# Seven block products in place of eight in six of the eight feed-forward blocks of both MLPs, and eight of fourteen modulation blocks moved into the attention

## The chip, the cores and the metric

One Trainium2 chip, one of its cores. The kernel is one launch. The metric is the device time of an execution in microseconds (us), read as the median of several executions. TensorE (PE) does the matrix products, VectorE (DVE), ScalarE (ACT) and GpSimd (POOL) the element-wise work, and SyncE (SP) issues nearly all DMA transfers from its own queue.

## What is computed

A two-layer trunk over 512 tokens of width 1024, batch 1, all in float32. Each layer is a token mixer and then an MLP, and each of these four sub-layers n = 0..3 is modulated by a vector c:

```python
shift, scale, gate = split(silu(c) @ ada_w[layer, s] + ada_b[layer, s], 3)   # gate is 1 + gate
u = x * (1.0 + scale) + shift
y = square(relu(u @ mlp_w1[layer] + mlp_b1[layer])) @ mlp_w2[layer] + mlp_b2[layer]   # s == 1: the MLP
x = layer_norm(ALPHA * x + gate * y, ln_g[layer, s], ln_b[layer, s])
```

`mlp_w1` is 1024 x 4096, `mlp_w2` 4096 x 1024, `ada_w[layer, s]` 1024 x 3072. The mixer of layer 0 joins a gated recurrence and linear attention heads. The mixer of layer 1 is an attention of 16 heads of 64 with a forget gate.

## The kernel before

**Products in three parts.** Every operand of a large product is held as a pair: `hi`, the float32 value rounded to the `fp32r` type (a copy on ACT), and `lo`, what the rounding left (a subtraction, mostly on DVE). A product is three matmuls, hi·hi, hi·lo and lo·hi, accumulated in PSUM (`mm3`). Each of them has a stationary operand of 128x128 and, in the MLPs, a moving one of 128x512.

**Stages in order of time.** The even mixer, its output projection (`mix_out(0)`), `mlp(0)`, the attention (`fox`), `mix_out(1)`, `mlp(1)`.

**An MLP.** `up(b)` makes block b of eight: 512 of the 4096 hidden channels for all 512 tokens, 4 groups f of 128 channels, each 24 matmuls. ACT takes relu and square from PSUM (`r`, then `hh`), DVE squares once more (`h2`) and subtracts for `hl`. `down(b)` multiplies these 512 tokens x 512 channels with rows b·512 to b·512+511 of `mlp_w2`, 96 matmuls of 128x512, and DVE adds the eight results from PSUM to `Y`. The order is up(0), then up(b), down(b-1) in turn, then down(7).

**Weights.** `plan_weights` lists all weight blocks of 1 MB in the order of use. `w_pre` loads the next ones to one of two staging tiles (`ws`, `WS_BUFS`) and splits one block: ACT writes `wh`, DVE `wl`. The split pairs stand in a rotation of four tiles each of 128x1024 (tags `wh`, `wl` of pool `wp`), or, for every second pair of blocks (`wsmall`, set by `alternate`), as 128x512 tiles from the general pool `s2`, which has 42 tiles (`S2_BUFS`). A third pool, `u8`, has eight tiles of 128x4x512.

**Modulation.** A block is 512 columns of one `ada_w[layer, s]`, a job (n, cb). `ada_steps` is a generator over jobs, four pieces each. A piece is two DMA loads of 128x512 (`ast`) and two multiply-adds into `acc`. There are two generators, stepped together by `tick()`: "v" does its multiply-adds on DVE (SCALAR_TENSOR_TENSOR, the first of a job TENSOR_SCALAR), "g" scales on ACT and adds on POOL. Two pieces into the next job, `finish` sums over the partitions with matmuls against ones (`pada`). Where `halved` is set the sum is first split in a pair (`acch`, `accl`), except for the last job of a generator. Shift and scale rows go through DRAM (`mod_d`), gates stay in SBUF for n = 1 and 3 and go through DRAM for n = 2 (`gate_d`). Six jobs run in the even mixer. Of the other fourteen, twelve run in mlp(0) and two, the gate of n = 3, in mlp(1), started at b = 1.

**Attention.** `fox` walks through 16 heads with the orders "aduntu3uv" and the like: a is the scores and softmax of the next head, d the decay tables (`Dm`, POOL) two heads ahead, n the normalisation (POOL), t the transposes of the probabilities (`ppt`, then `Ph` on ACT and `Pl` on DVE), v the values, digits the stacking of q and k. u is `run()`: one of 52 projection units (36 for q, k and v of head groups 1 to 3, each 24 matmuls of 128x256, then 16 for the gate, 12 of 128x512 each), which fill PE between the small products of the heads. The residual tables are prepared in single steps by `step()`, which takes from `self.later`.

**Order.** The program order above gives priorities. When the program is built a planner lays out, for each engine, a fixed order: the earliest work in program order whose inputs and tiles are free by its own estimates. On the chip each engine and the SP queue follow that order and wait at semaphores.

Of the kernel before, what the change touches and what calls it, by code (L numbers as in the profile page):

```python
# [36 lines left out]
PRED = mybir.dt.uint32  # L37

# [35 lines left out]
class Trunk:  # L74
# [26 lines left out]
    def setup(self):  # L101
        nc, i, c = self.nc, self.i, self.const
        self.ident = c.tile([P, P], F32, name="ident")
        make_identity(self.tc.nc, self.ident)
        self.ones = c.tile([P, P], F32, name="ones")
        nc.vector.memset(self.ones, 1.0)
        self.ones_r = c.tile([P, P], F32R, name="ones_r")
        nc.vector.tensor_copy(self.ones_r, self.ones)
        self.eps = c.tile([P, 1], F32, name="eps")
        nc.gpsimd.memset(self.eps, LN_EPS)  # L110

        crow = c.tile([KC, P], F32, name="crow")
# [21 lines left out]
        self.gate_d = {2: self.dram.tile([1, D], F32, name="gated2")}  # L134
# [79 lines left out]
    def ada_steps(self, jobs, eng, halved):  # L214
# [22 lines left out]
        def finish(n, cb, *acc):  # L237
# [8 lines left out]
            else:  # L246
                h = cb - 4
                if n == 2:
# [7 lines left out]
                if n == 2:  # L256
                    nc.sync.dma_start(self.gate_d[n][:, h * 512:h * 512 + 512], g)
# [58 lines left out]
    def plan_weights(self):  # L316
# [5 lines left out]

        def out(w, n):
# [4 lines left out]
        def mlp(l):  # L328
            w1, w2 = i["mlp_w1"][l], i["mlp_w2"][l]
            up = lambda b: [("ch", w1, b * 512, 256), ("ch", w1, b * 512 + 256, 256)]  # L330
            dn = lambda b: [("rows", w2, b * 512, 2 * l + 1), ("rows", w2, b * 512 + 256, 2 * l + 1)]
            L.extend(up(0))
# [3 lines left out]

        self.wsmall = set()

        def alternate(n0):
            for q in range(n0, len(L)):  # L340
                if (q - n0) // 2 % 2:
                    self.wsmall.add(q)

        n0 = len(L)
        out(i["ev_w_out"][0], 0)
        mlp(0)
        alternate(n0)
# [7 lines left out]
        out(i["od_w_out"][0], 2)  # L355
        mlp(1)
        alternate(n0)
# [3 lines left out]
    def w_dma(self):  # L361
        d = self.wlist[self.n_dma]
        kind, w = d[0], d[1]
        if kind == "ch":
# [34 lines left out]
    def w_pre(self, eng=None):  # L399
# [8 lines left out]
        kind = d[0]  # L408
        small = self.n_split in self.wsmall
# [18 lines left out]
        self.n_split += 1  # L428

# [668 lines left out]
    def mlp(self, l, X, rest, last):  # L1098
# [4 lines left out]
        def up(b):  # L1103
            hh, hl = self.u8("hh"), self.u8("hl")
            ws = self.w_take() + self.w_take()
# [10 lines left out]
            for f in range(4):  # L1116
                if b == 0:
# [3 lines left out]
                if f % 2 == 0:  # L1121
                    self.w_pre()
                col = 64 + l * 32 + b * 4 + f
                r, h2 = self.s2("r"), self.s2("h2")
                nc.scalar.activation(r, pts[f], AF.Relu, bias=self.colA[:, col:col + 1])
                nc.scalar.activation(hh[:, f], r, AF.Square)
                nc.vector.tensor_tensor(h2, r, r, op=ALU.mult)
                nc.vector.tensor_tensor(hl[:, f], h2, hh[:, f].bitcast(F32), op=ALU.subtract)
                if b:
                    self.step(2)  # L1130
                    if f % 2:
                        self.tick()
            return hh, hl

# [44 lines left out]
        Y = [[self.s2(f"Y{t}_{h}") for h in range(2)] for t in range(NT)]  # L1179
        prev = up(0)  # L1180
        for b in range(1, nb):
            if b == 1 and last:
                self.ada = [self.ada_steps([(3, 4)], "g", True), self.ada_steps([(3, 5)], "v", True)]
            cur = up(b)
            down(b - 1, *prev)
            prev = cur
        self.tick(99)
# [55 lines left out]
    def fox(self, rest):  # L1243
# [252 lines left out]
        def run(k=1):  # L1496
            for _ in range(k):
                f = next(units, None)
                if f:
                    f()  # L1500

# [57 lines left out]
    def run(self):  # L1559
# [3 lines left out]
        self.ada = [self.ada_steps([(1, 4), (2, 0), (2, 2), (2, 4), (3, 0), (3, 2)], "g", True),  # L1563
                    self.ada_steps([(1, 5), (2, 1), (2, 3), (2, 5), (3, 1), (3, 3)], "v", True)]
# [32 lines left out]
```

## Time and profile before

| | |
|---|---|
| median of three runs | 1263.32 us (1262.36 to 1264.07) |
| the profiled execution: its own time, its span | 1266.51 us, 1264.8 us |
| matmuls on PE | 6543, busy 1224.6 us |
| DVE, ACT, POOL busy | 908.8, 590.2, 512.9 us |
| HBM read | 172.10 MB |

All times in a row are us from the start of the span unless marked ns. Rows come from one profiled execution of the kernel before. In the trace every instruction carries one line, that of a helper (L50), so groups are told apart by the names of their tiles: `out<-in`.

### The profile page before, as it was taken

Reading aid. Unit: us, or ns where it says so; the run is one execution under the profiler, and the core shown is the slowest. Engines: PE = TensorE matmul, PEld = TensorE weight load, DVE = VectorE, ACT = ScalarE, POOL = GpSimd, SP = SyncE. Lnnn points to the kernel's source line nnn. Section 1 sums busy time; section 2 is a strip of 40 time slices with the busy share of each in tenths; the row PEclk is TensorE's granted clock in tenths of the full one; section 3 lists DMA queues with packets and bytes.
Section 4 is the critical chain, followed back from the end, with each engine's and each line's share of the span. In section 5 each row is a group of like instructions: output and inputs, shape, how many; then the busy total and the mean of one; then the engine's idle time right before and its main releaser. Section 6 shows DMA issues by size and latency. Waiting matters only on the chain. (4 is left out here: it accounts for less than half of the span.)

```text
span 1264.8 us, 17847 instructions
## 1 busy us (share of the span) xinstructions
PE 1224.6 (97%) x6543; PEld 1044.2 (83%) x6543; DVE 908.8 (72%) x1423; ACT 590.2 (47%) x1044; POOL 512.9 (41%) x524
## 2 busy tenths in 40 slices
PE   6999899999999999999999999999899999999997
PEld 5787678888888888888999999887888788888886
DVE  7689898768877866879578878778768744543656
ACT  3476653452453544432567767753453342322321
POOL 3665523346330321474266558558437000000166
PEclk9999999999999999999999999999999999999999
DMA  9657416163666466524232332343262624232311
GB/s 316 186 199 267 173 61 198 56 230 119 240 224 233 145 195 227 182 67 124 81 101 85 92 93 52 113 153 106 79 233 72 211 67 133 81 117 70 133 34 67
DMA packets 126409, 177.52 MB, mean 140 GB/s; under 512 B 9270, under 2 KB 82644, under 8 KB 126322
## 3 DMA queue, kind: packets, MB, share of 16 engines
q1 hardware_dynamic: 126210, 176.33, 42.4%
q8 instruction: 52, 0.85, 0.3%
q14 instruction: 35, 0.29, 0.1%
q10 hardware_dynamic: 112, 0.05, 0.0%
HBM read 172.10 MB, written 4.26 MB: 139 GB/s over the span
## 5 line engine op out<-in xcount | busy, mean ns | idle before, releaser
L50 DVE TENSOR_TENSOR wl<-ws,wh 128x512 fp32r<-128x512 f32 (+1 forms) x255 | 269.3, 1081 | 67.7 <-ACT wh L50 63.4
L50 ACT CAST wh<-ws 128x1024 fp32r<-128x1024 f32 (+2 forms) x271 | 207.5, 808 | 200.5 <-PE p L50 81.4
L50 PE MATMUL p<-uh,wh 128*128 128x512 f32 (+1 forms) x576 | 206.2, 366 | 0.0
L50 PE MATMUL p<-uh,wl 128*128 128x512 f32 (+1 forms) x576 | 205.9, 365 | 0.0
L50 PE MATMUL p<-wh,hh 128*128 128x512 f32 (+1 forms) x516 | 201.0, 390 | 0.0
L50 PE MATMUL p<-wh,hl 128*128 128x512 f32 (+1 forms) x516 | 200.0, 388 | 0.0
L50 PE MATMUL p<-wl,hh 128*128 128x512 f32 (+1 forms) x516 | 199.9, 387 | 0.0
L50 PE MATMUL p<-ul,wh 128*128 128x512 f32 (+1 forms) x576 | 192.9, 366 | 0.0
L50 POOL TENSOR_TENSOR acc<-acc,ast 128x512 f32<-128x512 f32 x70 | 102.9, 1470 | 203.3 <-ACT ast L50 108.4
L50 DVE TENSOR_TENSOR h<-r 128x512 f32<-128x512 f32 x64 | 53.6, 840 | 123.6 <-ACT r L50 123.6
L50 PEld LDWEIGHTS p<-uh,wl 128*128 128x128 f32 x576 | 108.6, 189 | 17.5
L50 PEld LDWEIGHTS p<-uh,wh 128*128 128x128 f32 x576 | 108.6, 189 | 17.6
L50 PEld LDWEIGHTS p<-ul,wh 128*128 128x128 f32 x576 | 100.9, 189 | 17.4
L50 PEld LDWEIGHTS p<-wh,hh 128*128 128x128 f32 x516 | 96.9, 188 | 20.3 <-issue 0.2
L50 PEld LDWEIGHTS p<-wl,hh 128*128 128x128 f32 x516 | 96.9, 188 | 20.2 <-issue 0.5
L50 PEld LDWEIGHTS p<-wh,hl 128*128 128x128 f32 x516 | 96.9, 188 | 19.8
L50 ACT ACTIVATE r<-p,colA 128x512 f32<-128x512 f32 x64 | 43.8, 684 | 148.7 <-PE p L50 148.7
L50 POOL TENSOR_TENSOR ws<-ws,gate 128x512 f32<-128x512 f32 x16 | 25.0, 1597 | 210.6 <-DMA ws<-in_mlp_w_dram 210.6
L50 DVE TENSOR_TENSOR Y<-Y,p 128x512 f32<-128x512 f32 x96 | 64.8, 681 | 41.0 <-PE p L50 40.3
L50 ACT ACTIVATE ast<-ast,cs 128x512 f32<-128x512 f32 x70 | 49.9, 721 | 91.3 <-DMA ast<-in_ada_w_dram 91.3
L50 DVE SCALAR_TENSOR_TENSOR acc<-ast,cs,acc 128x512 f32<-128x512 f32 x70 | 82.5, 1179 | 13.2 <-DMA ast<-in_ada_w_dram 12.7
L50 POOL TENSOR_TENSOR ul<-u,uh 128x512 fp32r<-128x512 f32 x32 | 45.0, 1418 | 74.0 <-ACT uh L50 65.4
(320 smaller groups left out, 2681.2 us busy)
## 6 DMA issues: line engine op xcount, KB each, us to landing
ws<-in_mlp_w_dram SPq DMA_DIRECT2D x64, 1024.0 KB
ast<-in_ada_w_dram SPq DMA_DIRECT2D x160, 256.0 KB
ws<-in_od_w_in_dram SPq DMA_DIRECT2D x16, 1024.0 KB
ast<-in_ada_w_dram SPq DMA_DIRECT2D x16, 512.0 KB
ws<-in_ev_w_in_dram SPq DMA_DIRECT2D x7, 1024.0 KB
ws<-in_ev_w_out_dram SPq DMA_DIRECT2D x4, 1024.0 KB
nf<-fd SPq DMA_DIRECT2D x16, 256.0 KB
ws<-in_od_w_out_dram SPq DMA_DIRECT2D x4, 1024.0 KB
```

Source lines behind the costliest of these rows:

```text
L50: x = f(*a, **k)
```

## The change

The pairs of blocks (0,1), (2,3), (4,5) of both MLPs take a new path (`WINOGRAD = (0, 1)` lists the layers). `up(b, raw=True)` keeps the squares as plain float32 (`hr`), with no `h2` and no `hl`. Two such tiles, 512 tokens x 1024 channels, are cut in 2x2 blocks of 256 tokens x 512 channels, and the 1024 x 1024 piece of `mlp_w2` in 2x2 blocks of 512 x 512. `winograd` multiplies seven combinations of them (Winograd's form of Strassen's scheme), each 4 x 2 x 3 = 24 matmuls of 128x512. `factor` makes the left operands (S1 to S4 by sums in place) and splits them. `wino_b` makes the right ones (T1 to T4 by sums in place in four `s2` tiles `wE` and in a staging tile) and splits them. `wino_dma` loads block B22 twice, once into `wE`. The seven results are accumulated in 12 `s2` tiles over the three pairs and put together by 8 additions per MLP. Blocks 6 and 7 go the old way, as up(6), up(7), down(6), down(7). The residual steps run one to a group from b = 2. The W1 blocks of the new path are split in the rotation of four, but for up(1) (and, as before, some of the last blocks).

The jobs (2,4), (2,5) and (3,0) to (3,5) are stepped in the attention, one tick to two projection units from the second `run()` on. mlp(0) keeps six jobs, mlp(1) none. All gates go through DRAM.

```diff
+WINOGRAD = (0, 1)
+WINO_B = ("B11", "T3", "T1", "T2", "B21", "T4", "B22")
+WINO_A = ("A11", "S3", "S1", "S2", "A12", "A22", "S4")
...
+            if l in WINOGRAD:
+                for g in range(0, 6, 2):
+                    L.extend(up(g) + up(g + 1) + [("wino", w2, g * 512, x) for x in WINO_B])
+                L.extend(up(6) + up(7) + dn(6) + dn(7))
...
+        if which in WINO_SRC:
+            r, c = WINO_SRC[which]
+            st = self.wp.tile([P, 4, 512], F32, tag="ws", bufs=WS_BUFS, name="ws")
+            nc.sync.dma_start(st, block(r0 + 512 * r, 512 * c))
+        if which == "T3":
+            E = [self.s2(f"wE{k}") for k in range(4)]
+            for k in range(4):
+                nc.sync.dma_start(E[k], w[r0 + 512 + k * P:r0 + 512 + k * P + P, 512:1024])
...
+        elif which == "T3":
+            self.wE, self.wB12 = self.wE_next, st
+            for k in range(4):
+                sub(self.wE[k], self.wE[k], st[:, k])
+        if which == "T1":
+            for a in (0, 2):
+                x = self.wB12[:, a:a + 2, :]
+                sub(x, x, self.wB11[:, a:a + 2, :])
+                r += halves(self.wB12, a)
+            for k in range(4):
+                nc.vector.tensor_tensor(self.wE[k], self.wE[k], self.wB11[:, k], op=ALU.add)
+            return r
+        for a in (0, 2):
+            r += halves(self.wE if which in ("T3", "T2", "T4") else st, a)
+        if which == "B21":
+            for k in range(4):
+                sub(self.wE[k], st[:, k], self.wE[k])
...
+            if q % 3 < 2:
+                t = self.u8("ha", F32R, (2, 4, 256))
+                parts = [(slice(0, 4), t[:, 0], t[:, 1])]
+            else:
+                parts = [(slice(f, f + 2), *[self.s2(x, F32R).rearrange("p (k t) -> p k t", k=2) for x in ("hah", "hal")])
+                         for f in (0, 2)]
+            if name == "S3":
+                sub(a[1], a[0], a[1])
+            elif name == "S1":
+                sub(a[1], a[3], a[1])
+                nc.vector.tensor_tensor(a[0], a[0], a[1], op=ALU.add)
+            elif name == "S4":
+                sub(a[2], a[2], a[1])
...
+            for fs, hi, lo in parts:
+                nc.scalar.copy(hi, src[:, fs])
+                sub(lo, src[:, fs], hi.bitcast(F32))
...
+            plan = [("1", False, "U2", None), ("7", False, "Q7", None), ("5", False, "Q5", 1), ("6", False, "U2", None),
+                    ("1", True, "C11", 0), ("7", True, "D21", 0), ("5", True, "D12", 1)]
+            for q, (bank, on, to, bias) in enumerate(plan):
+                if len(ops) < min(q + 3, 7):
+                    ops.append(factor(WINO_A[len(ops)], H, len(ops)))
+                w = self.w_take()
+                self.w_pre()
...
+            for g in range(0, 6, 2):
+                H = [up(g, True)[0], None]
+                first = [factor(WINO_A[q], H, q) for q in range(2)]
+                H[1] = up(g + 1, True)[0]
+                winograd(g, acc, H, first)
...
+                    done.append(f)
+                    if len(done) % 2 == 0:
+                        self.tick()
+
+        done = []
+        self.ada = [self.ada_steps([(2, 4), (3, 0), (3, 2), (3, 4)], "g", True),
+                    self.ada_steps([(2, 5), (3, 1), (3, 3), (3, 5)], "v", True)]
...
-        self.ada = [self.ada_steps([(1, 4), (2, 0), (2, 2), (2, 4), (3, 0), (3, 2)], "g", True),
-                    self.ada_steps([(1, 5), (2, 1), (2, 3), (2, 5), (3, 1), (3, 3)], "v", True)]
+        self.ada = [self.ada_steps([(1, 4), (2, 0), (2, 2)], "g", True),
+                    self.ada_steps([(1, 5), (2, 1), (2, 3)], "v", True)]
```

## Rows read from the trace of the kernel before

**Rows 1.** The page: busy time of the engines, then busy tenths in 40 slices

```profile
PE 1224.6 (97%) x6543; PEld 1044.2 (83%) x6543; DVE 908.8 (72%) x1423; ACT 590.2 (47%) x1044; POOL 512.9 (41%) x524
...
PE   6999899999999999999999999999899999999997
...
DVE  7689898768877866879578878778768744543656
```

**Rows 2.** Windows, by stage: busy us of each engine (instructions), clock, DMA share, GB/s

```profile
178.00:240.00 62.00, 59.26 (x298) 49.43 (x298) 54.64 (x89) 26.98 (x49) 17.58 (x11) 1.00 0.44 145
...
280.00:540.00 260.00, 260.00 (x1148) 215.16 (x1147) 198.28 (x226) 116.96 (x181) 86.32 (x59) 1.00 0.57 190
...
638.00:772.00 134.00, 133.63 (x1076) 131.28 (x1075) 107.45 (x266) 96.64 (x204) 83.34 (x156) 1.00 0.29 86
772.00:858.00 86.00, 83.81 (x468) 72.43 (x467) 65.22 (x134) 52.76 (x114) 52.16 (x74) 1.00 0.35 117
904.00:1251.00 347.00, 345.73 (x1609) 288.79 (x1609) 191.44 (x252) 116.65 (x181) 84.41 (x61) 1.00 0.32 106
```

**Rows 3.** Windows of 20 us, same columns: 140:160, 880:900, 980:1000

```profile
140.00:160.00 20.00, 15.86 (x92) 12.14 (x92) 17.30 (x29) 12.77 (x24) 9.16 (x7) 0.91 0.25 82
...
880.00:900.00 20.00, 16.74 (x75) 13.57 (x74) 18.46 (x36) 8.77 (x18) 11.31 (x6) 0.91 0.46 151
...
980.00:1000.00 20.00, 18.73 (x78) 14.20 (x77) 15.12 (x20) 12.21 (x20) 2.91 (x2) 1.00 0.66 232
```

**Rows 4.** The chain that ended last: start us, us, what

```profile
995.14 255.74 PE p L50 x1128
```

**Rows 5.** Groups of DVE, 1000 to 1180 us, POOL idle: busy us, mean ns

```profile
L50 DVE TENSOR_TENSOR wl<-ws,wh 128x512 fp32r<-128x512 f32 x39 | 24.7, 685 | 0.0
L50 DVE TENSOR_TENSOR Y<-Y,p 128x512 f32<-128x512 f32 x35 | 23.9, 685 | 24.1 <-PE p L50 23.5
L50 DVE TENSOR_TENSOR wl<-ws,wh 128x1024 fp32r<-128x1024 f32 x16 | 19.6, 1222 | 7.6 <-ACT wh L50 7.0
```

**Rows 6.** Timeline of DVE in mlp(1): start us, us for all instructions of the row

```profile
999.67 3.10 DVE L50 TENSOR_TENSOR wl<-ws,wh 128x512 fp32r<-128x512 f32 x5
```

**Rows 7.** Groups of DVE, 280 to 540 us (mlp(0))

```profile
L50 DVE SCALAR_TENSOR_TENSOR acc<-ast,cs,acc 128x512 f32<-128x512 f32 x42 | 48.3, 1150 | 10.1 <-DMA ast<-in_ada_w_dram 9.7
L50 DVE TENSOR_TENSOR wl<-ws,wh 128x512 fp32r<-128x512 f32 x48 | 46.2, 979 | 3.7 <-ACT wh L50 3.7
...
L50 DVE TENSOR_SCALAR acc<-ast,cs 128x512 f32<-128x512 f32 x6 | 9.1, 1523 | 0.0
L50 DVE TENSOR_TENSOR accl<-acc,acch 128x512 fp32r<-128x512 f32 x10 | 6.4, 680 | 0.0
```

**Rows 8.** Timeline of PE where mlp(1) finishes its two jobs

```profile
991.23 0.39 PE L50 MATMUL p<-uh,wl 128*128 128x512 f32 x1
992.20 1.12 PE L50 MATMUL pada<-acc,ones 128*128 128x512 f32 x2 [0.58 <-POOL acc L50]
994.01 1.12 PE L50 MATMUL pada<-acc,ones 128*128 128x512 f32 x2 [0.69 <-DVE acc L50]
994.58 0.80 PE L50 MATMUL p<-wh,hh 128*128 128x512 f32 x1
```

**Rows 9.** Groups of ACT, 1000 to 1180 us

```profile
L50 ACT CAST wh<-ws 128x512 fp32r<-128x512 f32 x32 | 17.0, 615 | 0.0
L50 ACT CAST wh<-ws 128x1024 fp32r<-128x1024 f32 x16 | 16.9, 1055 | 54.5 <-PE p L50 54.5
```

**Rows 10.** Tile acc, whole span: duration ns min/median/max, first and last start

```profile
L50 POOL TENSOR_TENSOR acc<-acc,ast x70: 1264/1421/1843, 84.3 to 990.5; 128x512 f32<-128x512 f32 x70
L50 DVE SCALAR_TENSOR_TENSOR acc<-ast,cs,acc x70: 735/917/1784, 87.6 to 993.2; 128x512 f32<-128x512 f32 x70
```

**Rows 11.** Groups of DVE and of ACT, 640 to 790 us and 280 to 540 us

```profile
L50 DVE TENSOR_TENSOR wl<-ws,wh 128x1024 fp32r<-128x1024 f32 x18 | 26.2, 1471 | 5.7 <-ACT wh L50 5.6
L50 DVE TENSOR_TENSOR Pl<-ppt,Ph 128x512 fp32r<-128x512 f32 x22 | 14.4, 682 | 0.7 <-ACT Ph L50 0.6
...
L50 ACT ACTIVATE ast<-ast,cs 128x512 f32<-128x512 f32 x41 | 29.5, 722 | 61.5 <-DMA ast<-in_ada_w_dram 61.5
```

**Rows 12.** DMA, 280 to 540 us: GB/s in 40 slices, then issues

```profile
GB/s 1 3 28 296 108 312 351 367 76 88 262 159 318 358 111 8 250 178 365 331 84 80 94 253 185 379 291 85 90 158 167 318 337 154 134 27 202 204 220 184
...
ws<-in_mlp_w_dram SPq DMA_DIRECT2D x24, 1024.0 KB
ast<-in_ada_w_dram SPq DMA_DIRECT2D x88, 256.0 KB
```

More of the change, by code (lines that the diff above doesn't have):

```diff
@@ L37 @@
 PRED = mybir.dt.uint32
+WINOGRAD = (0, 1)
+WINO_B = ("B11", "T3", "T1", "T2", "B21", "T4", "B22")
+WINO_A = ("A11", "S3", "S1", "S2", "A12", "A22", "S4")
+WINO_SRC = {"B11": (0, 0), "T3": (0, 1), "B21": (1, 0), "B22": (1, 1)}
 class InOrder:
@@ L133, in setup @@
         self.mod_d = {n: self.dram.tile([1, 2 * D], F32, name=f"modd{n}") for n in range(1, 4)}
-        self.gate_d = {2: self.dram.tile([1, D], F32, name="gated2")}
+        self.gate_d = {n: self.dram.tile([1, D], F32, name=f"gated{n}") for n in (1, 2, 3)}
     def ada_bias(self):
@@ L321, in plan_weights, with alternate @@
               ("ch", win, 2048, 256), ("ch", win, 2304, 256), ("ch", win, 640, 128), ("ch", win, 768, 256)]
+        self.wsmall = set()
+        def alternate(n0):
+            for q in range(n0, len(L)):
+                if (q - n0) // 2 % 2:
+                    self.wsmall.add(q)
         def out(w, n):
@@ L335, in mlp @@
             L.extend(dn(7))
[L337 to L342, printed above, removed]
+            alternate(n0)
         n0 = len(L)
         out(i["ev_w_out"][0], 0)
+        alternate(n0)
         mlp(0)
-        alternate(n0)
         win = i["od_w_in"][0]
@@ L363, in w_dma @@
         kind, w = d[0], d[1]
+        if kind == "wino":
+            return self.wino_dma(*d[1:])
         if kind == "ch":
@@ L428, in w_pre, with wino_dma, wino_b, halves @@
         self.n_split += 1
+    def wino_dma(self, w, r0, which):
+        nc = self.nc
+        block = lambda r, c: w[r:r + 512, c:c + 512].rearrange("(k p) f -> p k f", p=P)
+        st = None
+        if which in WINO_SRC:
[6 more added lines that the diff above has]
+                nc.sync.dma_start(E[k], w[r0 + 512 + k * P:r0 + 512 + k * P + P, 512:1024])
+            self.wE_next = E
+        self.wstage[self.n_dma] = st
+        self.n_dma += 1
+    def wino_b(self, which, st):
+        nc = self.nc
+        sub = lambda o, a, b: nc.vector.tensor_tensor(o, a, b, op=ALU.subtract)
+        r = []
+        def halves(src, a):
+            hi, lo = [self.wp.tile([P, 2, 512], F32R, tag=x, name=x) for x in ("wh", "wl")]
+            if isinstance(src, list):
+                for j in range(2):
+                    nc.scalar.copy(hi[:, j], src[a + j])
+                    sub(lo[:, j], src[a + j], hi[:, j].bitcast(F32))
+            else:
+                nc.scalar.copy(hi, src[:, a:a + 2, :])
+                sub(lo, src[:, a:a + 2, :], hi.bitcast(F32))
+            return [(hi[:, j], lo[:, j]) for j in range(2)]
+        if which == "B11":
+            self.wB11 = st
+        elif which == "T3":
[15 more added lines that the diff above has]
+                sub(self.wE[k], st[:, k], self.wE[k])
+        return r
     def w_take(self):
@@ new lines, in winograd @@
+        def winograd(g, acc, H, first):
+            ops = list(first)
+            pts = {}
+            plan = [("1", False, "U2", None), ("7", False, "Q7", None), ("5", False, "Q5", 1), ("6", False, "U2", None),
[4 more added lines that the diff above has]
+                w = self.w_take()
+                self.w_pre()
+                if not on:
+                    pts[bank] = [self.ps("p2") for _ in range(2)]
+                for k in range(4):
+                    for t in range(2):
+                        tok = slice(t * P, t * P + P)
+                        lh, ll = [x[:, tok] for x in ops[q][k]]
+                        for n3, (x, y) in enumerate(((lh, w[k][0]), (lh, w[k][1]), (ll, w[k][0]))):
+                            nc.tensor.matmul(pts[bank][t], x, y, start=(not on and k == 0 and n3 == 0),
+                                             stop=(k == 3 and n3 == 2), skip_group_check=True)
+                ops[q] = None
+                for t in range(2):
+                    if (to, t) in acc:
+                        nc.vector.tensor_tensor(acc[to, t], acc[to, t], pts[bank][t], op=ALU.add)
+                        continue
+                    acc[to, t] = self.s2(f"{to}{t}")
+                    if bias is None:
+                        nc.vector.tensor_copy(acc[to, t], pts[bank][t])
+                    else:
+                        nc.vector.tensor_tensor(acc[to, t], b2[bias], pts[bank][t], op=ALU.add)
@@ L1178, in mlp @@
         b2 = self.bc(i["mlp_b2"][l:l + 1, :], f"b2{l}")
[L1179 to L1185, printed above, removed]
-            prev = cur
+        if l in WINOGRAD:
+            acc = {}
+            for g in range(0, 6, 2):
[3 more added lines that the diff above has]
+                winograd(g, acc, H, first)
+            for t in range(2):
+                for x, y in (("D12", "U2"), ("D21", "U2"), ("Q7", "Q5"), ("Q7", "U2")):
+                    nc.vector.tensor_tensor(acc[x, t], acc[x, t], acc[y, t], op=ALU.add)
+            Y = [[acc["C11", t], acc["D12", t]] for t in range(2)] + [[acc["D21", t], acc["Q7", t]] for t in range(2)]
+            del acc
+            self.gates[n] = self.bc(self.gate_d[n], f"gate{n}")
+            prev = up(6)
+            cur = up(7)
+            down(6, *prev)
+            prev = cur
+        else:
+            Y = [[self.s2(f"Y{t}_{h}") for h in range(2)] for t in range(NT)]
+            prev = up(0)
+            for b in range(1, nb):
+                cur = up(b)
+                down(b - 1, *prev)
+                prev = cur
         self.tick(99)
```

52 lines of the change are left out of this document (39 added, 13 removed).

## The prediction

> **What bounds the kernel now.** I read the page first: PE is busy 97% of the span and its slices are full except at the start, DVE stands at 72% [rows 1]. Next the windows by stage: in mlp(0) PE is busy all of 260 us while DVE works 198 of them; in mlp(1) it is busy 345.73 of 347 us with DVE at 191; in the attention (638 to 772) 133.63 of 134, with DVE at 107.45, ACT at 96.64, POOL at 83.34 [rows 2]. The chain says that this busy time is not idling in disguise: 1128 matmuls of 128x512 follow each other in 255.74 us, so 0.2267 us each, without a wait between [rows 4]. So wherever the change works, PE sets the end today, and taking matmuls away is worth their full pace, as long as no other engine becomes the later one. What must be read next is therefore DVE's room in the MLPs and in the attention.
>
> **Matmuls removed.** A pair of blocks now costs eight block products of 24 matmuls, afterwards seven. Three pairs, two MLPs: 6 x 24 = 144 matmuls, 144 x 0.2267 = 32.6 us [rows 4]. The page "TensorE: Matmul & The Clock Gate" of the Trainium skill (Back-to-back issue gap) has 215.7 ns for such a matmul; by it the saving would be 31.1 us. The measured pace decides.
>
> **The two jobs leave mlp(1).** There PE ended a group of up at 991.23 + 0.23 and began down at 994.58: 3.1 us, in which it ran four `pada` records [rows 8]. Taking about 0.5 us for each pair of them (a pair's row is 1.12 us, most of it the last one draining), 2 us were waiting for `acc`. That wait goes; the `pada` matmuls themselves run elsewhere (the count of last jobs, whose sums are not split, stays at four). -2.0 us.
>
> **DVE in a pair of blocks.** With POOL idle a 128x512 TENSOR_TENSOR lasts 685 ns, from SBUF and from PSUM alike, and one of 128x1024 1222 [rows 5]. Queued behind each other they overlap: five in 3.10 us, so (3.10 - 0.69) / 4 = 0.60 us apart [rows 6]; taking the same 85 ns off gives 1.14 us for 1024. A pair then costs DVE: splits of W1, 8 x 1.14 = 9.1; right operands, 8 x 1.14 (halves from staging tiles) + 12 x 0.60 (halves from `wE`) + 12 x 0.60 (sums in `wE`) + 2 x 1.14 (B12 - B11) = 25.8; left operands, five splits of 1.14, four parts of 0.60 and four sums of 1.14 = 12.7; 14 results from PSUM x 0.60 = 8.4. Together 56.0 us. PE needs 192 matmuls of up (43.5 us) and 168 of the products (38.1), 81.6 in all. In mlp(0) two ticks to an up add four pieces on DVE, 8 x 1.15 = 9.2 us [rows 7]. So DVE has room over a pair: 69% and 80%.
>
> It has none inside the products. A `wh`/`wl` pair comes free only when the matmuls four pairs back are done, and S1 needs the second up to be finished. What can be done before the products start is A11 and S3 (3.4), the W1 splits but for the next group's first block (6.8), B11 (2.3), the T3 sums (2.4), the first half of T3 (1.2) and B12 - B11 (2.3). The other 37.6 us must go into the 38.1 us of products, an even match. By hand, from the start of the products: S1's sums 1.4 to 3.9 (relu and square of the last group come first, about 1.4 us), the second half of T3 to 5.1, S1's parts to 6.6, T1's halves by about 9.5 (PE wants S1 and T1 at 10.9), `wE` + B11 and T2 by about 15 (wanted at 16.3), B21 after that. B21's load waits for B11's staging tile, so for `wE` + B11 at about 12; a 1 MB load at the 250 to 370 GB/s of the fuller slices [rows 12] is 3 to 4 us, so it stands at about 17 and is wanted at 21.8. Each operand is ready 1 to 5 us ahead. ACT has 1.06 us a copy of 1024 [rows 9], some 21 us of the 38: not the limit. I take 1.5 us of waiting to a group, as a match this even leaves some: 9 us for the six. The lower end is 0. The upper end is a head start that doesn't happen (T3 and B12 - B11 done inside): 37.6 + 5.9 = 43.5, 5.4 a group, 32 us. POOL disturbs little here: its adds in mlp(0) come with the ticks, which are all in up.
>
> The 1 MB that each group loads twice adds 6 MB beside a DMA of 190 GB/s in mlp(0) [rows 2]; hidden by the slack above. The 8 closing sums and the gate loads through DRAM lie under up(6) and up(7), 43.5 us; without that cover the sums would cost 8 x 0.60 = 4.8 us an MLP.
>
> **The eight jobs in the attention.** 32 pieces, 16 on DVE: 28 SCALAR_TENSOR_TENSOR and 4 TENSOR_SCALAR, at the mean of mlp(0), 28 x 1.15 + 4 x 1.52 = 38.3 us, 6 splits of `acc` at 0.60 = 3.6 [rows 7], and 4 gate rows at about the same, 2.4: 44 us, less about 2 for overlap. On POOL 28 x 1.42 = 40 us [rows 10], on ACT 32 x 0.72 = 23 us [rows 11] and some 6 for copies. The ticks run from the second to the 34th unit, the window 638 to 772. There DVE would come to 107.45 + 42 = 149.5 us of 134; POOL to 123, ACT to 126 [rows 2]. So DVE becomes the limit of this window, 15.5 us late at least at that price, since the pieces come ahead of later heads in program order and can't be put off. Behind them in DVE's queue wait the scores' maxima, `Pl` and the splits of q, k, v weights, and behind these PE. The 64 loads more on the SP queue stand ahead of some `nf` loads, which are due two heads later, some 25 us: hidden, and if not, POOL's `Dm` is late next.
>
> From both sides: at the shortest SCALAR_TENSOR_TENSOR, 735 ns [rows 10], the sum is 107.45 + about 27 = 134.5 of 134, which I put at +5, since a full engine leaves others waiting (between 178 and 240 us DVE stood at 88% and PE lost 2.7 of 62 us [rows 2]). At the mean price with DVE filled to 93%, 149.5 / 0.93 = 161, +27; if the instructions there slow down too, 5 more, +32. I take +18, near the mean price, because POOL will be busier than it was where that mean was measured.
>
> The page "GPSIMD Engine Reference" of the Trainium skill (Key points) says that POOL shares its SBUF interfaces with VectorE and that instructions with two SBUF inputs suffer. The trace agrees: with POOL idle a `wl` of 1024 took 1222 ns [rows 5], in the attention 1471, while `Pl`, with one input in PSUM, stayed at 682 [rows 11]. What that rule makes of this change is the first rival below.
>
> **Sum.** -32.6 - 2.0 + 9 + 18 = -7.6 us. The profiled execution took 1266.5 us (span 1264.8 and 1.7 around it), so 1258.9 by its own time; it lies 3.2 us over the median of the runs, and the same difference from 1263.3 gives 1255.7. I say 1255.
>
> **The rivals.**
> (a) The other side: DVE and POOL get in each other's way in the attention. With POOL at 123 of 134 us nearly each of the 28 meets it and pays near the longest seen, 1784 ns [rows 10]: 28 x 1.7 + 4 x 1.52 + 6 = 60 us, DVE at 167 of 134, +33. Then -34.6 + 9 + 33 = +7.4, 1270.7. It decides from an attention longer by 25.6 us on. For it: POOL's share there; against: half of the 70 so far took under 917 ns. Chance 0.19.
> (b) The products of the six groups are bound by DVE or by a buffer, 5.4 us or more a group: -34.6 + 32 + 18 = +15, 1279. For it: 37.6 against 38.1 us, two staging tiles, and a fixed order laid out on estimates. Such pauses would not cost the clock as a long one does: it was granted at 0.91 in the two windows where PE stood 3 to 4 us of 20 and at 1.00 where it lost 1.3 [rows 3]. Against: DVE is free for 20 us in the up ahead. Chance 0.15.
> (c) All is hidden: no wait in the groups and +5 in the attention: -29.6, 1233.7. For it: mlp(0) ran at 76% of DVE without losing a us of PE. Chance 0.16.
> (d) The terms cancel within 0.2% (2.5 us, about what a measurement of this kernel tells from no change): attention at +25 with 9 in the groups. 1263. Chance 0.08.
>
> My forecast, 1240 to 1260, has the rest, 0.42. Faster is forecast and (c), 0.58; same 0.08; slower (a) and (b), 0.34. The likeliest case's own range is 1240 to 1260. The range for 8 in 10 runs from (c)'s 1234 to just past (b)'s 1279: 1281.
>
> **What would show it.** PE records fall by 144 of 128x512 with a pace still 0.2267. In the products DVE is busy over 90% and PE's idle ends on `wl`, `ha` or `hal` by DVE, under 2 us a group; over 5 is (b). Between 638 and about 790 DVE is over 90% with `acc` rows at 1.1 us or more and PE's share falls from 99.7% to about 88%; an attention as long as before is (c), rows of `acc` near 1.7 us are (a). mlp(1) has no gap at its first down. The prediction is wrong if PE waits in the groups for a load (staging tiles) or if attention waits on `nf`.

## The result and the profile after

The changed kernel takes 1302.59 us (median of four runs, 1299.71 to 1305.57); beside it the kernel before took 1263.63 (1262.36 to 1264.07). The ratio is 1.0306, 95% interval 1.0282 to 1.0330: 39 us slower, where 8 us faster was forecast, and past the range's upper end of 1281. The profiled execution took 1305.57 us, the slowest of the four, its span is 1303.8; it lies 39.0 us over the span before, as the medians do. Helper line L50 is L55 here.

The page, busy times and slices, to be laid beside [rows 1]:

```profile
PE 1219.0 (93%) x6399; PEld 1030.5 (79%) x6399; DVE 1026.4 (79%) x1525; ACT 670.2 (51%) x1130; POOL 538.4 (41%) x524
...
PE   6999899999969999999979978899999999999997
...
DVE  7688888678798789876678888877866959759856
...
PEclk9999999999989999999989889899999999999999
```

PE has 144 matmuls fewer, as the change says, but its busy time fell by only 5.6 us: some of the rest ran slower. Slices of 32.6 us with less than 8 tenths show where: the 12th in mlp(0), the 21st and 24th in the attention; the clock is granted lower in the same places.

For a table by stage I take the start times of matmuls in the trace: the last `down` matmul of an MLP ends its stage, the first of an output projection ends the attention. Each kernel's figures are from its profiled execution.

| us | to mix_out(0) | mix_out(0) | mlp(0) | attention | mix_out(1) | mlp(1) | tail |
|---|---|---|---|---|---|---|---|
| before | 185.2 | 48.6 | 359.9 | 254.4 | 53.0 | 355.0 | 8.6 |
| after | 184.1 | 47.8 | 367.6 | 305.8 | 52.8 | 337.1 | 8.6 |

mlp(1) gained 17.9 us, mlp(0) lost 7.7 where some 12 were to be gained, and the attention lost 51.4 where I took 18.

**mlp(1).** The chain that ended last, beside [rows 4], and the window of the third pair's products:

```profile
1100.55 189.35 PE p L55 x834
```

```profile
1170.00:1210.00 40.00, 40.00 (x178) 33.10 (x178) 39.32 (x54) 20.79 (x28) 0.00 (x0) 1.00 0.37 121
```

0.2270 us a matmul: the pace is unchanged, and each one taken away is worth it. PE does not stop although DVE is full; the even match of the prediction holds while POOL is idle. From the start of the first product matmul to the end of the last, the three groups last 38.53, 40.51 and 38.99 us against 168 x 0.2267 = 38.1. Of the excess of 3.7 us, 1.8 are eight matmuls of `up` that PE's order has among the products, so 1.9 us are waiting, nearly all in the second group.

**mlp(0).** Its groups last 40.69, 56.07 and 43.25 us. Without the twelve matmuls of `up` among them that is 23.0 us too long: 1.7, 17.1 and 4.2. Of the 17.1, about 5 are matmuls at the half pace and the rest waiting. Two windows in that second group (362 to 418 us), the groups of DVE from 346 to 378, the timeline of POOL, and that of DVE at the point where POOL ends:

```profile
360.00:380.00 20.00, 14.61 (x55) 10.63 (x54) 20.00 (x14) 6.31 (x10) 17.57 (x10) 0.91 0.14 40
380.00:400.00 20.00, 15.11 (x50) 11.38 (x49) 20.00 (x28) 9.50 (x14) 0.00 (x0) 0.74 0.32 106
```

```profile
L55 DVE TENSOR_TENSOR wE<-wE,ws 128x512 f32<-128x512 f32 x6 | 10.4, 1772 | 0.0
...
L55 DVE TENSOR_TENSOR wl<-ws,wh 128x1024 fp32r<-128x1024 f32 x2 | 4.6, 2318 | 0.0
```

```profile
341.25 8.54 POOL L55 TENSOR_TENSOR X<-X,rA 128x512 f32<-128x512 f32 x4
349.76 1.74 POOL L55 TENSOR_TENSOR acc<-acc,ast 128x512 f32<-128x512 f32 x1
351.46 15.79 POOL L55 TENSOR_TENSOR X<-X,rB 128x512 f32<-128x512 f32 x8
367.20 10.68 POOL L55 TENSOR_TENSOR acc<-acc,ast 128x512 f32<-128x512 f32 x6
```

```profile
375.01 3.42 DVE L55 TENSOR_TENSOR wl<-wE,wh 128x512 fp32r<-128x512 f32 x2
378.36 0.68 DVE L55 TENSOR_TENSOR wE<-wE,ws 128x512 f32<-128x512 f32 x1
```

POOL works without a pause from 341 to 378 us: twelve residual steps on `X`, with seven additions of the jobs pushed between and behind them. In that time a DVE instruction with two inputs in SBUF costs 1772 ns where 685 stood [rows 5], 2318 where 1222 stood, 1.1 us more at either length; the moment POOL ends, the same instruction takes 0.68 again. DVE got 14 instructions done in 20 us. The granted clock then fell to 0.91 and 0.74, so the 50 and 55 matmuls of these windows also ran in part at the half pace. The page "GPSIMD Engine Reference" of the Trainium skill (Key points) says that POOL shares its SBUF interfaces with VectorE, and that it contends with DVE instructions that have two SBUF inputs; the trace agrees, 685 to 1772 ns.

**The attention.** Whole window, then three of its stretches:

```profile
600.00:905.00 305.00, 275.82 (x1868) 252.97 (x1867) 230.29 (x495) 194.73 (x394) 186.42 (x264) 0.93 0.43 141
660.00:680.00 20.00, 13.72 (x89) 12.80 (x88) 14.21 (x37) 10.19 (x27) 13.81 (x22) 0.83 0.35 119
760.00:780.00 20.00, 12.83 (x87) 11.29 (x86) 16.92 (x34) 11.20 (x23) 15.46 (x20) 0.83 0.58 184
800.00:820.00 20.00, 11.99 (x74) 10.30 (x73) 17.87 (x28) 11.89 (x25) 16.70 (x20) 0.75 0.44 142
```

No engine is full in any of them; between 660 and 680 each rests 29% of the time or more. DVE is at 230 of 305 us. In the attention of before (594 to 848 us) it was at 188, so its load grew by just the 42 us that I had reckoned, and yet the window is not filled. Nor did its instructions grow dear: groups of DVE between 638 and 840 us, beside [rows 7, 11]:

```profile
L55 DVE SCALAR_TENSOR_TENSOR acc<-ast,cs,acc 128x512 f32<-128x512 f32 x28 | 27.7, 990 | 2.1 <-DMA ast<-in_ada_w_dram 1.9
L55 DVE TENSOR_TENSOR wl<-ws,wh 128x1024 fp32r<-128x1024 f32 x18 | 24.4, 1359 | 6.4 <-ACT wh L55 6.3
```

990 ns against the 1150 that I reckoned with, 1359 against 1471 before. What happens instead is seen in the timelines of PE, POOL and DVE at one stop, and in the window over it:

```profile
667.78 0.94 PE L55 MATMUL ppt<-ident,Sm 128*128 128x128 f32 x2 [6.28 <-POOL Sm L55]
```

```profile
660.03 1.37 POOL L55 TENSOR_TENSOR acc<-acc,ast 128x512 f32<-128x512 f32 x1
661.38 2.62 POOL L55 TENSOR_SCALAR Dm<-nf,Fc 128x256 f32<-128x256 f32 x4
663.96 1.26 POOL L55 TENSOR_TENSOR acc<-acc,ast 128x512 f32<-128x512 f32 x1
665.18 1.93 POOL L55 TENSOR_SCALAR_AFFINE_SELECT Dm<-Dm 128x128 f32<-128x128 f32 x4
667.33 1.42 POOL L55 TENSOR_SCALAR Sm<-Sm,rc 128x128 f32<-128x128 f32 x3 [0.22 <-DVE rc L55]
```

```profile
662.51 0.28 DVE L55 TENSOR_SCALAR mx<-mx 128x4 f32<-128x4 f32 x1
662.70 0.74 DVE L55 SCALAR_TENSOR_TENSOR acc<-ast,cs,acc 128x512 f32<-128x512 f32 x1
...
665.17 0.84 DVE L55 SCALAR_TENSOR_TENSOR acc<-ast,cs,acc 128x512 f32<-128x512 f32 x1
...
666.18 0.78 DVE L55 SCALAR_TENSOR_TENSOR acc<-ast,cs,acc 128x512 f32<-128x512 f32 x1
...
667.05 0.17 DVE L55 RECIPROCAL rc<-mx 128x4 f32<-128x4 f32 x1
```

```profile
660.00:668.00 8.00, 1.72 (x14) 1.48 (x12) 7.87 (x24) 4.61 (x17) 7.75 (x12) 0.92 0.86 293
```

PE waits 6.28 us for the normalised `Sm`; POOL needs `rc` for it, and `rc` on DVE, 0.17 us of work, stands behind three job instructions (and other work) in a fixed order. POOL itself is free for `Sm` only 0.22 us before `rc` comes, since two additions of jobs, 2.6 us, stand ahead in its order too. The head's chain goes through ACT, DVE, POOL and back, and here it queues behind pieces of jobs on two of them; PE's own order is fixed too, so it stands, and after such stops its clock is granted at half for a while. The averages over 20 us hide that DVE and POOL hardly rest over the stop, 7.87 and 7.75 of 8 us. In the ten stops of PE over 1 us in the attention, 28.8 us together, DVE is busy 95% of the time and POOL 81%. From the start times of the matmuls: in the attention PE idled 42.0 us (9.1 before) and lost 12.8 at the half clock (none before).

### The profile page after: what moved, and what is told of

Its sections match the earlier page's. It is cut to its first block, busy times and chain, and to the rows that moved or that the text cites. A ratio compares the mean times of both kernels' runs of the same rounds, so it can differ in the third digit from the quotient of the medians.

```text
span 1303.8 us, 17732 instructions
## 1 busy us (share of the span) xinstructions
PE 1219.0 (93%) x6399; PEld 1030.5 (79%) x6399; DVE 1026.4 (79%) x1525; ACT 670.2 (51%) x1130; POOL 538.4 (41%) x524
## 5 line engine op out<-in xcount | busy, mean ns | idle before, releaser
L55 ACT CAST wh<-ws 128x1024 fp32r<-128x1024 f32 (+2 forms) x231 | 206.0, 919 | 230.3 <-PE p L55 120.2
L55 DVE TENSOR_TENSOR wl<-ws,wh 128x1024 fp32r<-128x1024 f32 (+1 forms) x215 | 250.2, 1183 | 90.1 <-ACT wh L55 86.2
L55 PE MATMUL p<-uh,wh 128*128 128x512 f32 (+1 forms) x576 | 206.2, 366 | 0.0
L55 PE MATMUL p<-uh,wl 128*128 128x512 f32 (+1 forms) x576 | 205.1, 365 | 0.0
L55 POOL TENSOR_TENSOR acc<-acc,ast 128x512 f32<-128x512 f32 x70 | 112.3, 1605 | 209.5 <-ACT ast L55 153.6
L55 PE MATMUL p<-ul,wh 128*128 128x512 f32 (+1 forms) x576 | 192.9, 366 | 0.0
L55 PE MATMUL p<-wh,ha 128*128 128x512 f32 x480 | 151.6, 393 | 0.5 <-DVE ha L55 0.5
L55 PEld LDWEIGHTS p<-uh,wl 128*128 128x128 f32 x576 | 108.6, 189 | 17.6
L55 PEld LDWEIGHTS p<-uh,wh 128*128 128x128 f32 x576 | 108.6, 189 | 17.4
L55 PEld LDWEIGHTS p<-ul,wh 128*128 128x128 f32 x576 | 100.9, 189 | 17.4
L55 PEld LDWEIGHTS p<-wh,ha 128*128 128x128 f32 x480 | 90.9, 190 | 20.1 <-DVE ha L55 0.9
L55 PE MATMUL p<-wl,ha 128*128 128x512 f32 x240 | 94.1, 395 | 6.8 <-DVE wl L55 6.7
L55 POOL TENSOR_TENSOR ws<-ws,gate 128x512 f32<-128x512 f32 x16 | 25.2, 1606 | 155.8 <-DMA ws<-in_mlp_w_dram 148.0
L55 DVE SCALAR_TENSOR_TENSOR acc<-ast,cs,acc 128x512 f32<-128x512 f32 x70 | 76.7, 1095 | 11.3 <-DMA ast<-in_ada_w_dram 10.9
L55 PE MATMUL pqk<-wh,uh 128*128 128x256 f32 x256 | 75.4, 295 | 0.0
L55 POOL TENSOR_TENSOR ul<-u,uh 128x512 fp32r<-128x512 f32 x32 | 44.6, 1406 | 74.3 <-ACT uh L55 71.5
L55 PE MATMUL pqk<-wl,uh 128*128 128x256 f32 x256 | 74.0, 289 | 0.0
L55 PE MATMUL pqk<-wh,ul 128*128 128x256 f32 x256 | 73.6, 288 | 0.0
L55 ACT ACTIVATE r<-p,colA 128x512 f32<-128x512 f32 x64 | 43.5, 683 | 53.5 <-PE p L55 51.7
L55 ACT CAST wh<-wE 128x512 fp32r<-128x512 f32 x72 | 41.8, 619 | 48.6 <-PE p L55 32.6
L55 PEld LDWEIGHTS p<-wl,ha 128*128 128x128 f32 x240 | 45.4, 189 | 18.3 <-DVE wl L55 8.9
L55 DVE TENSOR_TENSOR wl<-wE,wh 128x512 fp32r<-128x512 f32 x72 | 51.0, 746 | 10.2 <-ACT wh L55 10.2
```

Source lines behind the costliest of these rows:

```text
L55: x = f(*a, **k)
```

## The experiments

### The jobs without the new products (ada_only)

```diff
-WINOGRAD = (0, 1)
+WINOGRAD = ()
...
             for b in range(1, nb):
+                if b == 6:
+                    self.gates[n] = self.bc(self.gate_d[n], f"gate{n}")
```

> The eight jobs move into the attention, the MLPs keep their eight products. Theory (the added multiply-adds delay the heads by themselves): the attention, from the last product of the first MLP to the first of the next output projection, is about 305 us as in the changed kernel, against 254 before; mlp(0) is within 2 us of before, mlp(1) 2 us shorter; 1305 to 1318 us in all. Rival (the attention is long because of what the new MLP leaves to it: a late start, tiles, another order): 254 to 262 us for the attention, 1260 to 1268 in all.

Attention 304.2 us, mlp(0) 357.1, mlp(1) 351.5; 1308.88 us, ratio 1.0362 (1.0337 to 1.0387). The window over the attention:

```profile
591.00:895.00 304.00, 273.66 (x1870) 252.13 (x1870) 229.55 (x496) 195.28 (x396) 189.88 (x264) 0.94 0.43 141
```

The loss in the attention is the moved jobs' alone; the new products don't enter it. The eight jobs were worth 2.8 us in mlp(0) and 3.5 in mlp(1), and cost 50 where they went.

### The jobs' arithmetic made short (short_both, short_v, short_g)

But for the first of each job, the multiply-adds of the eight moved jobs work on 8 of 512 columns; loads, sums and the count of instructions stay. short_both does it for both generators, short_v for DVE's alone, short_g for ACT's and POOL's.

```diff
-nc.vector.scalar_tensor_tensor(acc, st, c, acc, op0=ALU.mult, op1=ALU.add)
+nc.vector.scalar_tensor_tensor(acc[:, :c1], st[:, :c1], c, acc[:, :c1], op0=ALU.mult, op1=ALU.add)
...
-nc.scalar.activation(st, st, AF.Copy, scale=c)
-nc.gpsimd.tensor_tensor(acc, acc, st, op=ALU.add)
+nc.scalar.activation(st[:, :c1], st[:, :c1], AF.Copy, scale=c)
+nc.gpsimd.tensor_tensor(acc[:, :c1], acc[:, :c1], st[:, :c1], op=ALU.add)
...
```

> The changed kernel, with the multiply-adds of the eight jobs in the attention done on 8 of 512 columns, but for the first of each job; all loads, tiles, instructions and waits stay. What it leaves out: most of the sums for the last gate of the attention layer and for the last MLP's modulation. Theory (the time that DVE, ACT and POOL spend on them): the attention falls from 306 to 256 to 268 us, 1252 to 1266 in all. Rival (the 64 loads on the SP queue or the tiles that they hold): the attention stays at 295 us or more, 1290 or more in all.

> The changed kernel, with the multiply-adds on DVE of the eight jobs in the attention done on 8 of 512 columns but for the first of each job; those on ACT and POOL in full. What it leaves out: most of half of these modulation sums. Both full gave an attention of 305.8 us, both short 281.0. Theory (DVE's time is what delays the heads): 282 to 288 us. Rival (POOL and ACT do it, by their own time and by holding up DVE): 298 us or more.

> As the run before it, with the multiply-adds on ACT and POOL short and those on DVE in full. Theory (DVE's time): an attention of 298 us or more. Rival (POOL and ACT): 282 to 288 us. If both of these runs come out near 293, the two add up.

Attention 281.0 us in short_both, 298.8 in short_v, 288.1 in short_g; one run each, 1278.11, 1298.13 and 1289.42. Windows over the attention, in this order:

```profile
598.00:879.00 281.00, 267.71 (x1871) 249.42 (x1870) 194.25 (x495) 183.84 (x395) 150.34 (x264) 0.96 0.46 153
```

```profile
598.00:896.00 298.00, 273.83 (x1868) 251.93 (x1867) 215.88 (x495) 194.41 (x394) 180.86 (x264) 0.94 0.43 144
```

```profile
600.00:887.00 287.00, 269.76 (x1867) 249.92 (x1866) 210.19 (x494) 183.50 (x394) 156.22 (x264) 0.95 0.45 149
```

Neither side of the first expectation was met: 24.8 us went away and 26.6 stayed. The two halves add up: 7.0 from DVE, 17.7 from ACT and POOL, 24.8 together. In both of the latter it was the rival, POOL and ACT, that came out. Shortening DVE's own multiply-adds gives the least, which speaks against my claim that DVE's load is the limit. But the two halves do not separate the engines: short_g takes 20 us of busy time off DVE as well, short_v 14. Beside short additions on POOL, DVE's full multiply-adds fall from 990 ns to 778, as the group of short_g from 600 to 887 us shows:

```profile
L55 DVE SCALAR_TENSOR_TENSOR acc<-ast,cs,acc 128x512 f32<-128x512 f32 x28 | 21.8, 778 | 1.7 <-DMA ast<-in_ada_w_dram 1.4
```

In short_both DVE was busy 194 of 281 us, nearly as little as in the attention of before (188), and PE still idled 22.6 us. Note that the planner lays out every variant anew, so single differences of a few us also hold a change of order: mlp(0), which none of the short variants touches, took 363.5 to 365.4 us in these three and 367.6 in the changed kernel.

### Loads and sums taken away as well (short_small, no_sums)

short_small is short_both with loads of 8 columns, but for the first of each job. no_sums also leaves out the `pada` matmuls of these jobs.

```diff
+m = c1 if r else 512
-nc.sync.dma_start(st, w[r * P:r * P + P, cb * 512:cb * 512 + 512])
+nc.sync.dma_start(st[:, :m], w[r * P:r * P + P, cb * 512:cb * 512 + m])
```

```diff
-pt = self.ps("pada")
-for q, a in enumerate(acc):
+pt = acc[0].bitcast(F32) if c1 < 512 else self.ps("pada")
+for q, a in enumerate(acc if c1 == 512 else ()):
```

> The changed kernel with the multiply-adds of the eight jobs in the attention on 8 columns, as in the run that gave an attention of 281.0 us, and with their loads cut to 8 columns too, but for the first of each job. What it leaves out: most of these modulation sums. Queue entries, tiles and waits stay. Theory (what was left of the loss is ACT and DVE standing at loads that land late, heads' work behind them): 258 to 268 us. Rival (what is left comes from tiles taken, queue entries and the order laid out): 277 us or more.

> As the run that gave an attention of 274.7 us (multiply-adds and loads of the eight jobs on 8 columns), and the jobs' sums over partitions left out as well: a row is copied from the split tile instead of from the matmuls' result, so no matmul of theirs stands in PE's order and none holds a PSUM bank until ACT has copied its row. What it leaves out: the modulation of the last gate of the attention layer and of the last MLP. Theory (the sums' own 4.5 us, and PE standing at them and at the bank that they hold): 260 to 267 us. Rival (the tiles that the jobs take and the order laid out around them): 271 us or more.

Attention 274.7 and 267.7 us; 1272.18 and 1269.21 us, one run each. The first lies between the two sides of its expectation, the second just above its theory's 267. Windows over it:

```profile
596.00:870.00 274.00, 263.55 (x1868) 244.86 (x1867) 199.32 (x495) 183.38 (x394) 146.95 (x264) 0.98 0.34 104
```

```profile
600.00:867.00 267.00, 259.46 (x1852) 241.87 (x1851) 194.69 (x491) 182.21 (x393) 150.75 (x264) 0.98 0.35 106
```

So of the 51.4 us, taken away in this order: 24.8 by the length of the arithmetic, 6.3 by the size of the loads, 7.0 by the sums on PE with their waits, and 13.3 are left when the jobs have nearly nothing to do. The 6.3 and the 7.0 come from single runs and are not far above the 4 us by which mlp(0) differs though nothing in it was changed. The 13.3 must be among what is left of the jobs, places in the queues, tiles, the first operation of each job, and the order; which, stays open. PE's idle time and its loss at the half clock went down together: 42.0 and 12.8 us after, 22.6 and 7.8 in short_both, 20.4 and 3.6 in short_small, 18.1 and 3.7 in no_sums.

### POOL's residual steps out of the products (late_resid)

```diff
-                if raw:
-                    self.step(b > 1)
-                elif b:
+                if b and not raw:
                     self.step(2)
```

> The changed kernel, with the residual steps taken out of the new ups, so that POOL does them in up(6). Theory (DVE and POOL hold each other up in the second group): the second group of mlp(0) falls from 56 us to 39 to 42, that of mlp(1) from 40.5 to 39; 1282 to 1288 us in all, if up(6) covers the steps as it covered them before. Rival (the second group is bound by DVE's own work and order): it stays over 50 us and the time is within 4 us of the changed kernel.

The second group of mlp(0) fell from 56.07 to 44.09 us, the groups of mlp(1) to 38.53, 38.53 and 38.99. But mlp(0) came to 375.0 us, the tail to 14.1, and the whole to 1317.70, ratio 1.0436 (1.0413 to 1.0459). The cause of the dear group is confirmed, although 44.09 lies a little over the 39 to 42 expected: with the steps gone from it, DVE's `wl` of 128x1024 is back at 1217 ns there (362 to 408 us). What I expected of the total was wrong; the longer tail was not followed up. That group of DVE, then timelines of POOL and PE in up(6):

```profile
L55 DVE TENSOR_TENSOR wl<-ws,wh 128x1024 fp32r<-128x1024 f32 x9 | 10.9, 1217 | 0.1
```

```profile
524.12 6.86 POOL L55 TENSOR_TENSOR X<-X,rB 128x512 f32<-128x512 f32 x4
530.95 2.27 POOL L55 TENSOR_TENSOR acc<-acc,ast 128x512 f32<-128x512 f32 x1
533.17 7.33 POOL L55 TENSOR_TENSOR X<-X,rB 128x512 f32<-128x512 f32 x4
540.46 6.72 POOL L55 TENSOR_TENSOR ws<-ws,gate 128x512 f32<-128x512 f32 x4
547.14 1.70 POOL L55 TENSOR_TENSOR acc<-acc,ast 128x512 f32<-128x512 f32 x1
548.81 6.26 POOL L55 TENSOR_TENSOR ws<-ws,gate 128x512 f32<-128x512 f32 x4
555.03 2.60 POOL L55 TENSOR_TENSOR acc<-acc,ast 128x512 f32<-128x512 f32 x2
```

```profile
557.68 3.78 PE L55 MATMUL pada<-acc,ones 128*128 128x512 f32 x4 [19.80 <-POOL acc L55]
```

The steps, and eight products `ws<-ws,gate` behind them, now stand between the additions of the last jobs, and PE, whose order has their sums ahead of down(6), waits 19.8 us, in which POOL's three additions take 4.3.

### The jobs back in the MLPs (back_late, back_spread, back_lazy)

All three keep the new products in both MLPs, put twelve jobs into mlp(0), one tick to a group f, and two into mlp(1). back_late has the steps in up(6) as in late_resid; back_spread has two to an up from up(2) to up(5); back_lazy is back_spread with the split of a job's sum and its `pada` matmuls each two ticks later.

```diff
+            if last:
+                self.ada = [self.ada_steps([(3, 4)], "g", True), self.ada_steps([(3, 5)], "v", True)]
...
-                if b and f % 2:
+                if b:
                     self.tick()
...
```

```diff
-                    self.step(b > 1)
+                    self.step(b > 1 and f % 2 == 0)
```

```diff
-            if done and r2 == 2:
+            if done and r2 == 2 and not halved:
...
+            if wait and r2 == 0:
+                finish(*wait)
+                wait = None
...
```

> The new products in both MLPs, residual steps in up(6), and all jobs where they were before: twelve in mlp(0), one tick after each group of an up, two in mlp(1). Theory (the products are worth their 16 us an MLP where DVE keeps up, and the attention was the loss): attention 254 to 257 us, mlp(1) 337 to 341, mlp(0) 345 to 356; 1233 to 1248 in all. Rival (DVE in mlp(0) is full with twelve jobs beside the products): mlp(0) at 368 us or more, 1257 or more in all.

> The new products in both MLPs, all jobs where they were before (one tick after each group of an up), and the residual steps spread over up(2) to up(5), two to an up. Theory (POOL's work, when it stands in one block, doubles the DVE instructions beside it and holds up the sums of the last jobs; spread it fits): mlp(0) 350 to 366 us, attention 254, mlp(1) 337 to 341; 1240 to 1258 in all. Rival (twelve jobs are too much for mlp(0) with the products, however POOL's work lies): mlp(0) at 385 us or more, 1275 or more.

> New products in both MLPs, all jobs in the MLPs, residual steps spread, as in the run that gave 403 us for mlp(0); here a job's sums over partitions are issued two ticks later (its split at the last piece of the next job, the matmuls at the first piece of the one after). Theory (PE's order holds the products behind sums whose adds on POOL and DVE are late): mlp(0) falls to 362 to 380 us, 1258 to 1276 in all. Rival (the adds are late by any measure, or the products wait for DVE anyway): mlp(0) at 392 us or more, 1288 or more.

| | mlp(0) | attention | mlp(1) | tail | whole, us | ratio |
|---|---|---|---|---|---|---|
| back_late | 410.8 | 254.1 | 339.7 | 15.1 | 1307.17 | 1.0353 (1.0329 to 1.0377) |
| back_spread | 403.1 | 254.5 | 344.3 | 8.6 | 1299.61 | 1.0298 (1.0276 to 1.0319) |
| back_lazy | 399.4 | 254.8 | 343.5 | 8.6 | 1293.35 | 1.0231 (1.0208 to 1.0254) |

The attention is back at 254 us in all three, as expected, and the loss stands in mlp(0) instead, where each time the rival came out; in back_spread mlp(1), at 344.3, missed the 337 to 341 expected as well. Waits of PE in mlp(0) of back_spread, then of back_lazy (us, times, longest):

```profile
PE pada L55 <- ACT acch L55: 22.4, 4, 15.2
PE pada L55 <- DVE accl L55: 12.1, 6, 6.6
PE pada L55 <- POOL acc L55: 5.4, 1, 5.4
```

```profile
PE pada L55 <- DVE accl L55: 15.6, 5, 6.6
PE p L55 <- ACT hah L55: 10.9, 2, 8.3
PE pada L55 <- ACT acch L55: 9.3, 2, 4.8
```

39.9 us of waiting for the sums of jobs in back_spread. The theory that their place in PE's order is what is wrong fell with back_lazy: two ticks later PE still waits 24.9 us in the rows shown, 10.9 come up at an operand, and mlp(0) gains only 3.7 us. Shown is that twelve jobs beside the new products cost mlp(0) 39.5 to 50.9 us in these three orders. That the additions themselves are late because DVE (busy 345 of 401 us in mlp(0) of back_lazy, 274 of 360 before), ACT and POOL give the products their time is argued, not shown.

### The new products in mlp(1) alone (wino1, wino1_late)

wino1 has `WINOGRAD = (1,)`, twelve jobs in mlp(0) and two in mlp(1) as before. wino1_late also moves the residual steps of mlp(1) from up(2) to up(4):

```diff
-                    self.step(b > 1)
+                    self.step(b > 3)
```

> The new products in mlp(1) alone; mlp(0) and all jobs as before (two jobs in mlp(1), stepped from up(1) on). Theory (the products are worth their matmuls where POOL is idle, and the losses came from the attention and from mlp(0)): mlp(1) 337 to 341 us against 355, the rest as before; 1243 to 1250 us in all. Rival (the gain in mlp(1) came only with the two jobs gone, or mlp(1) passes waits on from elsewhere): mlp(1) at 346 us or more, 1255 or more.

> The new products in mlp(1) alone, jobs as before, and the residual steps of mlp(1) from up(4) on in place of up(2). In the run before it PE stood 12 us before the second group, at the sums of the two jobs, which waited for POOL's adds behind the residual steps. Theory (that queue on POOL is the whole loss): no gap there, mlp(1) at 338 to 342 us, 1245 to 1251 in all. Rival (the sums are late for another reason, their loads or ACT): a gap of 8 us or more stays, 1256 or more.

wino1: 1260.71 us, ratio 0.9978 (0.9963 to 0.9993), with mlp(1) at 352.7. Its groups last 40.61, 39.86 and 38.99, so they were not the cost. The rival's number came out. Its reason did so in part: PE stands at a sum of the two jobs, but they need not leave, as the next run shows. Timelines of POOL and PE in the second pair's ups:

```profile
1018.55 15.66 POOL L55 TENSOR_TENSOR X<-X,rB 128x512 f32<-128x512 f32 x8
1034.18 5.04 POOL L55 TENSOR_TENSOR acc<-acc,ast 128x512 f32<-128x512 f32 x3
```

```profile
1039.27 3.78 PE L55 MATMUL pada<-acc,ones 128*128 128x512 f32 x4 [11.63 <-POOL acc L55]
```

Eight steps on `X` hold back the last additions of a job, and PE stands 11.6 us for the job's sum. wino1_late moves the steps out of the job's way: `pada` waits for nothing, mlp(1) takes 341.7 us (the third group, just behind the moved steps, now lasts 42.04), the whole 1252.12 (1248.31 to 1254.83, six runs; 1 us over the expected 1251), ratio 0.9899 (0.9877 to 0.9922). The window of mlp(1):

```profile
899.00:1241.00 342.00, 338.39 (x1595) 282.74 (x1593) 262.15 (x316) 158.88 (x229) 97.46 (x66) 1.00 0.36 120
```

This version beats both kernels: 11.5 us, or 1.0%, under the one before, 50 under the changed one.

## Why the prediction was wrong, step by step

**Matmuls removed, -32.6: right.** 144 records fewer at 0.2270 us. In mlp(1) -16.3 from them and -3.1 from the stop at the sums [rows 8], against +1.9 of waiting, make -17.5; measured -17.9.

**The two jobs' wait, -2.0: right in place**, and worth the whole stop of 3.1 us, the four `pada` included.

**The groups, +9: wrong in mlp(0).** Measured are 24.9 us for the six, 1.9 in mlp(1) (0.6 a group, less than the 1.5 taken) and 23.0 in mlp(0) (7.7 a group, half pace included). The step that failed is "POOL disturbs little here: its adds in mlp(0) come with the ticks, which are all in up". The additions were run late, into the products, and the twelve residual steps of POOL, which the change itself puts one to a group from b = 2 on, I had not counted at all. My working of the even match has no room for a DVE at half its speed over 20 us. late_resid shows this for the second group (56.07 to 44.09 us). In the first group PE waits 1.4 us at `wl`, in the third 3.3 at `hal` and `ha`, all by DVE; why DVE is late there was not followed up. Rival (b) put 32 us on the groups, but by DVE's own work or a buffer, and named no POOL.

**The attention, +18: wrong, and outside my own bounds of 5 and 32.** The step that failed is "So DVE becomes the limit of this window". I added up each engine's load and looked for one that went over, DVE at 149.5 of 134; measured, none did. The loads were right (42 us more on DVE); what failed is the step from a load over the whole window to the time. DVE was busy 120.6 of the 152 us from 638 to 790, yet PE's idle time in the attention grew by 32.9 us and 12.8 more went at the half clock: DVE is full for a few us at a time, with POOL often full beside it, and PE stands just then. short_v speaks against DVE's own added work as the whole of it: without its long multiply-adds 44.4 of the 51.4 us stay. How much of the 17.7 us of short_g comes by ACT and POOL, and how much by the DVE that they let go faster, no run separates. Rival (a), dearer instructions, is refuted by the 990 ns. What I left out is the latency of a head's chain through three in-order queues with foreign work in each, and what PE's stops do to its clock. I had the warning in hand, PE at 0.91 where it stood 3 to 4 us of 20 [rows 3], and used it only to say what such pauses would not cost in the groups. Shown: the loss is that of the jobs alone (ada_only, and the attention at 254 us whenever they are back), about half goes with the length of their arithmetic, more of that with the part on ACT and POOL than with DVE's. Argued from timelines, and not shown for each stop: that the queues are the way by which it acts. Open: 13.3 us.

**Sum.** -32.6 - 3.1 + 24.9 + 51.4 = +40.6 us; measured by stage, +39.0 in the two profiled spans. The stages around are 2.1 us shorter, mlp(1) is 0.4 shorter and mlp(0) 1.0 longer than these terms have them. That the six jobs leave mlp(0) has no term in the prediction: ada_only puts it at -2.8 us. About 4 us go the other way at 548 to 554 us, where PE waits 1.9 us for a job's sum and then runs at the half clock for 3.4.

Of the signs named in advance, the records, the pace and the missing stop in mlp(1) were as said. DVE over 90% from 638 to 790 did not show (79%), and that alone would have told, without an experiment, that the theory of the attention had fallen. Nor did the two signs of a late load: PE's waits in the groups end on `wl`, `ha`, `hal` and `hah`, and POOL waited for `nf` less in the attention than before (16.6 us against 33.2).

## What to carry to other kernels

An engine's free time in a stage is room only for work that no one waits behind: where a latency chain (here a softmax through ACT, DVE and POOL) runs through in-order queues, price added work by what it puts ahead of the chain, not by the sum of busy times, and look what PE's clock does when it stops. A share of 70% over 20 us can hide an engine that is full just while PE waits for it. Where DVE has no slack, count every POOL instruction that falls into the same stretch, residual steps and the like too, wherever program order puts them. A saving of PE time is best taken where the other engines have room: the same products were worth 13.3 us in mlp(1) of wino1_late, where POOL's steps are kept out of their way. In mlp(0), beside six jobs and the steps, they cost 10.5 us (367.6 against 357.1 in ada_only, which has the same jobs there). wino1_late, without those, takes 0.9899 of the time before.

## What was not expected of the hardware

The price of POOL's work to DVE is not a share of the instruction but, at the two lengths seen, the same 1.1 us for each one with two SBUF inputs while POOL runs back to back: 685 to 1772 ns for 128x512, 1222 to 2318 for 128x1024. And spells at the half clock were a cost of their own, 12.8 us of the attention's 51, although PE's longest stop there was 6.3 us; where PE was full, as from 1170 to 1210, the clock was granted at 1.00.
